# A two-layer decoder trunk on one core: the last layer-norm table loaded earlier, attention masks added on VectorE, state-space tables made dense and spread by ScalarE, and the first weight chunks in pieces

## Chip, cores, metric

One Trainium2 chip, one of its cores. The time is the device time of one execution in microseconds (us); less is better. Before the change it is 2101.03 us, the median of three runs (2099.38, 2101.03, 2104.73).

## What is computed

Two layers over 256 tokens of width 2048, all in float32:

```python
for i in range(DEPTH):                       # DEPTH = 2
    if i % 2 == 0: mix = _even_mixer(x, ...) # u, q, k, v, gate from one projection;
                                             # 8 heads of forgetting attention (causal, with a
                                             # cumulative log gate), a diagonal complex state-space
                                             # layer (S5) with GELU and GLU, one output projection
    else:          mix = _odd_mixer(x, ...)  # 32 query heads, 4 key heads, window 128, sinks, rotary
    x = _layer_norm(ALPHA * x + mix, ...)
    ffn = _conv_ffn(x, ...)                  # 2048 -> 2 x 5504, causal conv of width 3, silu gate, -> 2048
    x = _layer_norm(ALPHA * x + ffn, ...)
```

In the windowed attention the scores outside the band are minus infinity, and the sink of a head is one more logit of its softmax:

```python
s = jnp.where(valid[None, :, None, None], s, -jnp.inf)
p = jax.nn.softmax(jnp.concatenate([s, sink], axis=-1), axis=-1)[..., :-1]
```

## The kernel before

**Weights.** Nearly all time is matmuls with weights that are read once. `Stream` brings them in as chunks, 128 partitions by 1024 columns (512 KB), in the order of the list `items`: SyncE issues the load into a ring of five buffers (`raw`), ScalarE copies the chunk to `hi`, rounded to the matmul's format (L115), VectorE subtracts (`lo = raw - hi`, L120), and TensorE multiplies in three passes: hi with the high half of the activations, hi with the low half, lo with the high half. So 128 rows of a contraction are three matmuls in a row, and one chunk with 512 columns of output is 12. At most `HELD` = 4 chunks are held as hi and lo; chunks whose destination is named ("x", or a place that is free at that time) go there instead. A destination "H" means chunks half as wide (512 columns), cast into a second, narrow set of buffers that `second_buffer` opens.

**Order.** Every engine runs its instructions in the order of the program text as it is executed; there is no scheduler. Work beside the stream comes from generators: after each chunk `done` casts further chunks, as far as there is room, and then `pump` gives each generator a step, which lasts until the costs that the generator yields add up to its budget (`step`, 1.7 for the state-space layer, `S5_BUDGET`), or until it yields 0. So the text's order sets, on each engine, what stands ahead of a cast.

**Stages**, by the timeline: u (16 chunks of wu, to 55 us, tiles of 128 output columns, each from two chunks); the gate (wf, one small chunk) and v (16 chunks of wv) to about 107; q and k with the attention heads, then the output projection's first part, to about 300; GLU and the rest of layer 1's mixer to about 430; its feed-forward net to 1112; layer 2's projections and windowed attention to 1312 and its output projection wo1; the second feed-forward net from 1398; the last down projection's tail and the final layer norm from 2060 on. Between the layers `boundary` runs a layer norm under the matmuls.

**u.** TensorE makes u in two groups of four tiles, for each group first the upper half of the contraction of all four, then the lower. x comes in eight pieces behind the first chunk. A finished tile is copied by ScalarE (L1385) and stored to a scratch tensor (L1386); after each second tile `load_u4` reads the pair back, transposed, with four DMAs that GpSimd issues (L1365).

**State-space layer** (`s5_gen`), one of four groups b after another: `tab` multiplies a phase table with B or C (four products over 128x512 in `z0` to `z3`, then four sums and differences, each over 64 partitions, straight into a sparse, block-diagonal table); `turn` and `kernels` take it through TensorE; GpSimd makes the powers ("phasors", L302 to L304) of which `phase` (six VectorE steps) makes the phases of group b; `toeplitz` fills a table with blocks of a kernel `gs`: four additions with the skip matrix on VectorE and six copies on ScalarE (L1144); `scan` does the recurrence; `emit` the outputs. `weave` places TensorE's parts after a given number of VectorE's steps (`WEAVE`).

**Windowed attention** (`Swa`, `scores` and `soft`), 16 head pairs: six matmuls of q and k into two banks, of 256 and 512 columns, and after each three one matmul of the identity with a mask (`maskr`); two reductions to the negated maximum (L833, L834), a minimum with the sink, and four exponentials on ScalarE from the banks, with their sums (L841). Its output projection wo1 has its chunks of the columns 0 to 1535 from the 17th on as "H".

**The end.** `final` (after the second feed-forward net) opens a buffer, loads scale and bias of the last layer norm, 2 MB, on ScalarE's queue (`load_gb`, L576), and then runs the last eight chunks for each half of the tokens, and the norm.

## Time and profile before

| | us |
|---|---|
| median of three runs | 2101.03 |
| the profiled execution | 2106.23 |
| its span in the profile | 2104.4 |
| TensorE busy | 2071.1 |
| VectorE busy | 1485.5 |
| ScalarE busy | 1144.9 |
| GpSimd busy | 70.7 |

Times of the profile are microseconds from the span's start. PE is TensorE's matmul, PEld its weight load, DVE VectorE, ACT ScalarE, POOL GpSimd, SP SyncE; a trailing q (SPq) is an engine's DMA queue. A row has an engine, a line of the kernel, an operation, and "out<-in" by the names of the tiles without their numbers; a tile without a name is `t`. `bank` is a bank of PSUM. Matmuls overlap, so their durations (0.39 us for 512 columns) add up to more than the time that passes; what one costs is the time from its start to the next one's. In square brackets stands how long the engine sat idle before the row, and what released it.

### The profile page before, as it was taken

How to read it: one execution, taken by the hardware profiler on the slowest of the kernel's cores; microseconds unless marked ns; L12 is line 12 of the kernel's file. 1: busy time of each engine (PE TensorE's matmuls, PEld its weight loads, DVE VectorE, ACT ScalarE, POOL GpSimd, SP SyncE). 2: the span in 40 equal slices, each digit the busy share in tenths (PEclk: the TensorE clock that was granted, in tenths of full speed). 3: DMA queues.
4: the chain of work that ended last, by engine and by line, in shares of the span. 5: the costliest groups of instructions: out<-in, count | busy, mean ns of one | idle time of the engine just before them, and what ended most of it. 6: DMA issues, size and time to landing. Idle time of an engine off the chain costs nothing.

```text
span 2104.4 us, 30826 instructions
## 1 busy us (share of the span) xinstructions
PE 2071.1 (98%) x11228; PEld 1761.9 (84%) x11228; DVE 1485.5 (71%) x2473; ACT 1144.9 (54%) x1920; POOL 70.7 (3%) x140
## 2 busy tenths in 40 slices
PE   8999999999999999999999999999999999999996
PEld 8788878888888888888888877788888888888885
DVE  7898867788777777655557876778777777755555
ACT  5445545665555555544446665475555555544442
POOL 4700000000000000000000000000000000000000
PEclk9999999999999999999999999999999999999998
DMA  8454455576666666466675643657666666646664
GB/s 288 149 166 140 128 194 184 180 220 201 189 189 192 190 189 188 150 188 197 194 240 164 185 127 102 219 182 223 190 189 192 189 190 187 193 148 194 193 193 176
DMA packets 133640, 388.92 MB, mean 185 GB/s; under 512 B 15536, under 2 KB 17584, under 8 KB 133232
## 3 DMA queue, kind: packets, MB, share of 16 engines
q1 hardware_dynamic: 126288, 371.38, 56.7%
q10 hardware_dynamic: 5712, 10.20, 1.9%
q0 software_dynamic: 1488, 5.38, 0.8%
q8 instruction: 88, 1.44, 0.3%
q14 instruction: 64, 0.52, 0.1%
HBM read 383.75 MB, written 3.15 MB: 184 GB/s over the span
## 4 chain that ended last, share of the span: by engine, by line
PE 87%; DVE 5%; DMA 3%; POOL 2%; ACT 2%; issue 1%; SPq 0%; DVEq 0%; ACTq 0%; POOLq 0%
PE bank L242 85%; DVE lo L120 2%; ACT hi L115 1%; DMA raw<-wdn 1%; DVE z L221 1%; DVE t L239 1%; DMA xraw<-xT 1%; POOL t L303 1%; POOL t L304 1%; POOL t L302 1%; DMA t<-ut 1%; DVE t L221 0%; PE bank L521 0%; DMA raw<-wo 0%; DMA raw<-wu 0%
## 5 line engine op out<-in xcount | busy, mean ns | idle before, releaser
L120 DVE TENSOR_TENSOR lo<-raw,hi 128x1024 fp32r<-128x1024 f32 (+1 forms) x828 | 842.7, 1022 | 473.9 <-ACT hi L115 472.8
L242 PE MATMUL bank<-t,hi 128*128 128x512 f32 (+1 forms) x3296 | 1101.1, 385 | 6.9 <-ACT t L115 6.1
L115 ACT CAST hi<-raw 128x1024 fp32r<-128x1024 f32 (+1 forms) x831 | 737.0, 891 | 587.9 <-PE bank L242 323.0
L242 PE MATMUL bank<-t,lo 128*128 128x256 f32 x3152 | 875.9, 278 | 0.9 <-DVE lo L120 0.9
L242 PEld LDWEIGHTS bank<-t,hi 128*128 128x128 f32 x3296 | 610.1, 188 | 138.5 <-ACT t L115 6.1
L242 PE MATMUL bank<-hi,t 128*128 128x512 f32 x2248 | 712.6, 393 | 0.7 <-ACT hi L115 0.7
L242 PEld LDWEIGHTS bank<-t,lo 128*128 128x128 f32 x3152 | 593.2, 188 | 1.8 <-DVE lo L120 1.6
L242 PEld LDWEIGHTS bank<-hi,t 128*128 128x128 f32 x2248 | 422.6, 188 | 94.6 <-issue 3.8
L242 PE MATMUL bank<-lo,t 128*128 128x512 f32 x1124 | 439.7, 391 | 2.0 <-DVE lo L120 2.0
L242 PEld LDWEIGHTS bank<-lo,t 128*128 128x128 f32 x1124 | 211.5, 188 | 47.7 <-DVE lo L120 3.8
L239 DVE SCALAR_TENSOR_TENSOR y<-h,t,y 128x255 f32<-128x255 f32 (+1 forms) x328 | 136.4, 478 | 0.6 <-ACT y L661 0.5
L439 ACT COPY h<-bank 128x256 f32<-128x256 f32 x164 | 60.6, 373 | 88.4 <-PE bank L242 86.0
L661 ACT ACTIVATE y<-h,t 128x256 f32<-128x256 f32 x164 | 90.3, 602 | 13.2 <-DVE h L221 13.0
L242 PE MATMUL bank<-t,t 128*128 128x512 f32 (+3 forms) x422 | 85.6, 349 | 2.1 <-DVE t L239 1.1
L221 DVE TENSOR_TENSOR h<-h,bank 128x256 f32<-128x256 f32 x164 | 67.0, 421 | 21.2 <-ACT h L439 21.2
L242 PEld LDWEIGHTS bank<-t,t 128*128 128x128 f32 (+1 forms) x422 | 61.8, 173 | 14.3 <-DVE t L120 2.2
L841 ACT ACTIVATE p<-bank,sm 128x128 f32<-128x128 f32 (+1 forms) x64 | 26.1, 420 | 45.1 <-DVE sm L221 45.1
L670 ACT ACTIVATE y<-y 128x256 f32<-128x256 f32 x86 | 35.6, 414 | 19.1 <-DVE y L239 19.0
L525 ACT ACTIVATE x<-bank,t 128x128 f32<-128x128 f32 x96 | 36.1, 457 | 10.7 <-PE bank L521 9.3
L245 ACT CAST t<-y 128x256 fp32r<-128x256 f32 x86 | 34.6, 404 | 5.2 <-DVE y L221 5.2
L221 DVE TENSOR_TENSOR t<-y,t 128x256 fp32r<-128x256 f32 x86 | 35.8, 418 | 0.9 <-ACT t L245 0.9
L221 DVE TENSOR_TENSOR y<-y,y 128x256 f32<-128x256 f32 x86 | 35.8, 419 | 0.3 <-ACT y L670 0.3
(172 smaller groups left out, 969.4 us busy)
## 6 DMA issues: line engine op xcount, KB each, us to landing
raw<-wup SPq DMA_DIRECT2D x328, 512.0 KB, 3.7
raw<-wdn SPq DMA_DIRECT2D x292, 256.0 KB, 3.0
raw<-wo SPq DMA_DIRECT2D x56, 512.0 KB, 3.6
raw<-wi SPq DMA_DIRECT2D x40, 512.0 KB, 3.8
raw<-wqk SPq DMA_DIRECT2D x32, 512.0 KB, 3.5
raw<-wdn SPq DMA_DIRECT2D x22, 512.0 KB, 5.1
raw<-wu SPq DMA_DIRECT2D x16, 512.0 KB, 6.4
raw<-wv SPq DMA_DIRECT2D x16, 512.0 KB, 4.1
```

The source lines that it names most:

```text
L115: self.nc.scalar.copy(hi, r)
L120: eng.tensor_tensor(lo, r, hi.bitcast(F32), op=ALU.subtract)
L221: V.tensor_tensor(o, a, b, op=op)
L239: V.scalar_tensor_tensor(o, a, s, b, op0=op0, op1=op1)
L242: PE.matmul(o, lhsT=l, rhs=r, start=start, stop=stop)
L245: S.copy(hi, src)
L302: G.tensor_tensor(t1, a[0], b[i], op=ALU.mult)
L439: S.copy(o, ps[:, T:])
L525: S.activation(x32[:, j], pt[:, j * P:(j + 1) * P], AF.Identity, bias=lnT[:, li, 1, k:k + 1], scale=lnT[:, li, 0, k:k + 1])
L661: S.activation(y[e], ps[e][:, :T], AF.Identity, bias=cw[:, n, 3:4], scale=cw[:, n, 2:3])
L670: S.activation(y[0], y[0], AF.Silu)
L841: S.activation(pp[:, e], vv[:, e], AF.Exp, bias=sm[:, 0, qb, e:e + 1], scale=1.0, accum_out=sm[:, 2, qb, e:e + 1])
```

## The change

It has seven parts.

1. `final` no longer loads the scale and bias. `Ffn.run` does, in the second column block of the last down projection, into the buffer of the transposed activations (`last_gb`).
2. `scores` has no mask matmuls. VectorE adds the mask, which lies in the constants, takes the maximum and writes the sum to SBUF in one `tensor_tensor_reduce` for each head and query block; the sink is its start value. The exponentials work in place.
3. wo1 has only chunks of 1024 columns in the common ring; `second_buffer` isn't opened for it.
4. `tab` makes dense sums and differences over 128 partitions (two instead of four operations), and ScalarE spreads them into the sparse table with four copies. `z0` and `z2` have two buffers. `toeplitz` adds the skip matrix once, in place, and ScalarE copies all ten blocks. The forgetting attention's probabilities are scaled by ScalarE.
5. A generator's rest of budget is carried to its next step (up to twice the budget), for the state-space layer with 1.45 instead of 1.7; `WEAVE` and the first group's places are smaller by what `tab` has lost.
6. The first two chunks of u are loaded and cast in four and two pieces, the first one's between the pieces of x, and four matmuls on zeros go ahead.
7. u's eight tiles are made at once, in eight banks: the upper half of the contraction for all, then the lower half.

```diff
-S5_BUDGET = 1.7
+S5_BUDGET = 1.45
-WEAVE = 2, 3, 5, 7, 8, 11
+WEAVE = 2, 3, 5, 6, 7, 9
...
     def step(self, ent):
         gen, budget = ent
-        spent = 0.0
-        while spent < budget:
+        credit = min(budget + self.credit.get(gen, 0.0), 2 * budget)
+        while credit > 0:
...
+    def piece(i, c, n):
+        m = CH // n
+        items.append((A["wu"][i, 0][:, c * m:(c + 1) * m], m, ("x", ...
+    for h in range(2):
+        for i in range(8):
+            if h == 0 and i < 2:
+                for c in range(4 - 2 * i):
+                    if i == 0:
+                        xchunk(c)
+                    piece(i, c, 4 - 2 * i)
...
-            own = ("H",) if n1 >= 12 + HELD and cc < 3 else None
-            w("wo1", cc, kp, dst=ext("t2", kp, own) if cc == 3 else own)
+            w("wo1", cc, kp, dst=ext("t2", kp) if cc == 3 else None)
...
+    for _ in range(4):
+        PE.matmul(ip[:, :T], lhsT=idle[:, :P], rhs=idle, start=True, stop=True)
...
+                if self.l == 1 and cc == 1:
+                    self.gb = last_gb(3)
...
-            gb = mk(lp, [P, 2, D])
-            load_gb(gb, li, 0, 4)
+        gb, part = ffn.gb, []
...
-                mm(s0, identr, maskr[:, :, 1, :], False, True)
-                mm(s1, identr, maskr.rearrange("p e b k -> p e (b k)"), False, True)
...
+                        V.tensor_tensor_reduce(out=pp[:, e], in0=vv[:, e], in1=cst[:, c:C_CM + P], scale=-1.0,
+                                               scalar=nsk[:, 1, h + e:h + e + 1], op0=ALU.add, op1=ALU.min,
+                                               accum_out=sm[:, 0, qb, e:e + 1])
...
+            for i, f in enumerate((sub, add)):
+                d = x4[2 * i]
+                f(d, d, x4[2 * i + 1])
                 yield 0.6
+                for hf in range(2):
+                    r = slice(64 * hf, 64 * hf + 64)
+                    S.copy(dst[r, i, :, :, 16 * hf:16 * hf + 16], d[r])
...
         def toeplitz(b):
             gs = cell["gs"]
+            add(gs[0:32], gs[0:32], dz[b])
+            yield 0.4
             for q in range(4):
                 for l in range(3 - q, 4):
                     k = l - 3 + q
-                    o = tm[32 * q:32 * q + 32, :, l, :]
-                    if k == 0:
-                        add(o, gs[0:32], dz[b])
-                    else:
-                        S.copy(o, gs[32 * k:32 * k + 32])
-                yield 0.35
+                    S.copy(tm[32 * q:32 * q + 32, :, l, :], gs[32 * k:32 * k + 32])
+                yield 0.1
...
-        ts(pr[:, 0:P], pr[:, 0:P], sm[:, 2, 0:1], ALU.mult)
+        S.mul(pr[:, 0:P], pr[:, 0:P], sm[:, 2, 0:1])
...
-    for i0 in (0, 4):
-        ps = [bank(acc) for _ in range(4)]
-        for c in range(2):
-            for i in range(i0, i0 + 4):
+    ps = [bank(acc if i < 4 else aux) for i in range(8)]
+    for c in range(2):
+        for i in range(8):
```

Three places in the engines' order show what moves. GpSimd, from the loads of the first state-space constants to the first phasors; u_39 and u_42 are the first two pairs of u tiles. Before:

```order
L971 DMA cz_219<-sCz 128x512
L971 DMA dz_220<-sDz 32x256
L1365 DMA u_39_411<-t_164 32x8x64 x4
L1365 DMA u_42_500<-t_164 32x8x64 x4
L302 ISA
L302 TENSOR_TENSOR t_197<-t_197 128x32
```

The change, the same place and, after the line of dots, 24 rows on; the pairs are u_45 and u_48:

```order
L996 DMA dz_247<-sDz 32x256
L1388 DMA u_45_588<-t_187 32x8x64 x4
L309 ISA
L309 TENSOR_TENSOR t_224<-t_224 128x32
...
L310 TENSOR_TENSOR t_224<-t_224 128x32
L311 TENSOR_TENSOR t_224<-t_224 128x32
L1388 DMA u_48_696<-t_187 32x8x64 x4
L309 TENSOR_TENSOR t_231<-t_230,t_224 128x64
```

The second pair's reads have moved from ahead of the phasors to among them.

ScalarE at the end of the v projection, from the cast of chunk 27 (counted from 0) to that of chunk 28. `hi` is a chunk's cast, `gs` the kernel that `toeplitz` copies, the rows of 128x256 and 8x256 the forget gate's tables, and 128x512 the copies of v. Before:

```order
L115 CAST hi_1294<-raw_1080 128x1024
L1301 CAST t_1032<-t_1036 128x256
L1302 CAST t_1033<-t_1036 128x256
L245 CAST t_1034<-bank_1300 128x256
L1305 CAST t_1032<-t_1034 8x256
L1306 ACTIVATE t_1033<-t_1034 8x256
L1305 CAST t_1032<-t_1035 8x256
L1306 ACTIVATE t_1033<-t_1035 8x256
L1144 COPY t_207<-gs_1167 32x8x32 x6
L1410 COPY t_964<-bank_965 128x512
L1410 COPY t_964<-bank_966 128x512
L115 CAST hi_1351<-raw_1140 128x1024
```

The change, from the row behind the cast of chunk 26 to the cast of chunk 28:

```order
L1167 COPY t_234<-gs_1189 32x8x32 x10
L116 CAST hi_1329<-raw_1115 128x1024
L1324 CAST t_1059<-t_1063 128x256
L1325 CAST t_1060<-t_1063 128x256
L252 CAST t_1061<-bank_1335 128x256
L1328 CAST t_1059<-t_1061 8x256
L1329 ACTIVATE t_1060<-t_1061 8x256
L1328 CAST t_1059<-t_1062 8x256
L1329 ACTIVATE t_1060<-t_1062 8x256
L1440 COPY t_984<-bank_985 128x512
L1440 COPY t_984<-bank_986 128x512
L116 CAST hi_1378<-raw_1174 128x1024
```

The Toeplitz copies, ten instead of six, stand ahead of the cast of chunk 27 instead of that of chunk 28.

TensorE at the first head pair's scores; `qT` rows are the products with q, `hi` and `lo` rows those of the weight stream, and t_110 with t_109 the identity with the mask. Before:

```order
L242 MATMUL bank_11440<-hi_11423,t_77 128x512
L242 MATMUL bank_11511<-t_11030,qT_11458 128x256 x3
L242 MATMUL bank_11511<-t_110,t_109 128x256
L242 MATMUL bank_11512<-t_11030,qT_11458 128x512 x3
L242 MATMUL bank_11512<-t_110,t_109 128x512
L242 MATMUL bank_11439<-hi_11453,t_77 128x512
```

The change:

```order
L249 MATMUL bank_11480<-lo_11464,xT_77 128x512
L249 MATMUL bank_11480<-hi_11463,xT_77 128x512
L249 MATMUL bank_11551<-t_11070,qT_11498 128x256 x3
L249 MATMUL bank_11552<-t_11070,qT_11498 128x512 x3
L249 MATMUL bank_11479<-hi_11493,xT_77 128x512
```

The two mask rows are gone, and the stream's next chunk follows the scores at once.

More of the change, by code (lines that the diff above doesn't have):

```diff
@@ L163, in step @@
             if c == 0:
-                return
-            spent += c
+                break
+            credit -= c
+        if gen in self.credit:
+            self.credit[gen] = credit
     def pump(self):
@@ L409, in trunk @@
     identr = mk(const, [P, P], F32R)
-    maskr = mk(const, [P, 2, 2, P], F32R)
+    maskr = mk(const, [P, P], F32R)
     def consts_round():
         S.copy(identr, ident)
-        for e in range(2):
-            S.copy(maskr[:, e, 0, :], cst[:, C_BM:C_BM + P])
-            S.copy(maskr[:, e, 1, :], cst[:, C_CM:C_CM + P])
+        S.copy(maskr, cst[:, C_CM:C_CM + P])
     spare = mk(const, [P, 1])
@@ L423, in warm @@
         S.activation(spare, spare, f)
+    idle = mk(st.xraw, [P, T])
+    V.memset(idle, 0.0)
+    ip = bank(aux)
+    for _ in range(4):
+        PE.matmul(ip[:, :T], lhsT=idle[:, :P], rhs=idle, start=True, stop=True)
     def bmm(ps, hi, lo, k, first, last):
@@ L713, in resid, with last_gb, final, half @@
                 residual(self.ps, 3, (tb,))
[L715 to L744 removed]
+    def last_gb(li):
+        t_ = mk(xtp, [P, KT * 2 * T], tag="xT")[:, :2 * D].rearrange("p (i d) -> p i d", i=2)
+        load_gb(t_, li, 0, 4)
+        return t_
+    def final(ffn):
+        gb, part = ffn.gb, []
+        def half(tb):
+            ffn.resid(tb, 7)
+            steps = ln_stats(tb)
+            next(steps)
+            for c in range(0, D, 256):
+                o = x[:, tb, c:c + 256]
+                stt(o, o, lnw[:, tb, 0:1], gb[:, 0, c:c + 256], ALU.subtract, ALU.mult)
+                next(steps, None)
+            for _ in steps:
+                pass
+            c = 0
+            for n in (512, 512, 512, 256, 256):
+                o = x[:, tb, c:c + n]
+                stt(o, o, lnw[:, tb, 2:3], gb[:, 1, c:c + n], ALU.mult, ALU.add)
+                nc.sync.dma_start(out=out[:, tb, c:c + n], in_=o)
+                c += n
+        for tb in range(2):
+            for c in range(8):
+                if tb == 0:
+                    part.append(st.get())
+                ffn.tail(part[c], tb, c)
+            half(tb)
     rope = mk(const, [P, 2, 2, 8])
@@ L1037, in four @@
         def four(tag="z"):
-            return [mk(wk, [P, 512], tag=f"{tag}{i}") for i in range(4)]
+            return [mk(wk, [P, 512], tag=f"{tag}{i}", bufs=2 - i % 2) for i in range(4)]
         def tab(dst, sc, src, b):
@@ L1226, in s5_gen @@
             if b == 0:
-                yield from weave(tables, (2, turn, 0, 0), (4, turn, 0, 1), (5, kernels, 0, 0), (6, kernels, 0, 1), (8, kernels_turn))
+                yield from weave(tables, (2, turn, 0, 0), (3, turn, 0, 1), (4, kernels, 0, 0), (5, kernels, 0, 1), (6, kernels_turn))
                 while b not in u4:
@@ L1242, in s5_gen @@
             if b < 3:
-                yield from weave((tab(wbs, sb, bt[b + 1], b + 1),), (4, emit, b))
+                yield from weave((tab(wbs, sb, bt[b + 1], b + 1),), (3, emit, b))
             else:
@@ L1528, in trunk @@
     ffn2.hs.close()
-    final(ffn2, 3)
+    final(ffn2)
     ffn2.outer.close()
```

118 lines of the change are left out of this document (48 added, 70 removed).

## The prediction

> **What bounds the kernel now.** I read the page first, then the busy time by stages, then TensorE's timeline at the places where it is not full. The busy totals and the engines of the chain that ended last:
>
> ```profile
> PE 2071.1 (98%) x11228; PEld 1761.9 (84%) x11228; DVE 1485.5 (71%) x2473; ACT 1144.9 (54%) x1920; POOL 70.7 (3%) x140
> PE 87%; DVE 5%; DMA 3%; POOL 2%; ACT 2%; issue 1%; SPq 0%; DVEq 0%; ACTq 0%; POOLq 0%
> ```
>
> TensorE is busy for 98% of the span, so time can go in two ways only: by matmuls that are no longer issued, and by idle stretches of TensorE that close. The stages that the change touches (columns: stretch, length, then busy time and count of PE, PEld, DVE, ACT, POOL, granted clock, DMA share, GB/s):
>
> ```profile
> 58.00:160.00 102.00, 97.68 (x623) 81.86 (x622) 92.68 (x153) 47.58 (x79) 38.07 (x72) 1.00 0.51 158
> 1148.00:1313.00 165.00, 165.00 (x814) 131.09 (x813) 120.02 (x258) 97.96 (x251) 0.00 (x0) 1.00 0.46 137
> 2060.00:2104.00 44.00, 28.40 (x111) 22.00 (x109) 27.18 (x61) 8.07 (x9) 0.00 (x0) 0.83 0.45 170
> ```
>
> In the attention stage (1148 to 1313) TensorE has no gap at all and VectorE 45 us of them. In the state-space stage (58 to 160) TensorE misses 4.3 us and VectorE is the fullest other engine. At the end TensorE stands for a third of the time, at a clock of 0.83.
>
> **The end.** TensorE's timeline there (start, length, last column the idle time and its releaser), then the piece of the chain ahead of it and the two groups of DMA issues:
>
> ```profile
> 2070.01 2.89 PE L242 MATMUL bank<-t 128*128 128x512 f32 x12
> 2076.22 0.79 PE L242 MATMUL bank<-t 128*128 128x512 f32 x1 [3.32 <-ACT t L115]
> 2077.48 3.78 PE L242 MATMUL bank<-t 128*128 128x512 f32 x8 [0.47 <-DVE t L120]
> 2087.25 4.93 PE L242 MATMUL bank<-t 128*128 128x512 f32 x21
> ...
> 2064.46 10.64 DMA raw<-wdn
> ...
> t<-ln ACTq DMA_DIRECT2D x1, 2048.0 KB, 10.7
> ...
> raw<-wdn SPq DMA_DIRECT2D x292, 256.0 KB, 3.0
> ```
>
> `load_gb` in `final` puts 2 MB on ScalarE's queue just when the last weight chunks are asked for. A chunk takes 10.64 us to land, TensorE waits 3.32 and 0.47 us and then goes at half speed: 8 matmuls in 3.78 us, 0.47 each, where later 21 take 4.93, 0.235 each. Without the 2 MB the chunk lands before TensorE has finished its 12 matmuls at 2072.90. From 2076.22 up to 2087.25 it issues 33; at 0.235 they take 7.75 us from 2072.90 and end at 2080.65. **Gain: 2087.25 - 2080.65 = 6.6 us.**
>
> The load goes to the second column block of the last down projection, where chunks of 256 KB stream, six matmuls each. I bound what it does there by two loads of 2 MB: the one above, 6.6 us with its cold clock, and this one in the output projection, with the weight chunks beside it (at other times they take 3.6 us by the page):
>
> ```profile
> raw<-wo SPq DMA_DIRECT2D x4, 512.0 KB, 4.3
> t<-x POOLq DMA_DIRECT2D x1, 2048.0 KB, 10.6
> ```
>
> There no matmul waited. A place with a full ring of chunks ahead is nearer to that one. **Cost: 0 to 6.6, I take 1.4 us.**
>
> **The masks.** 32 matmuls leave the attention scores, half of 512 columns, half of 256:
>
> ```profile
> L242 PE MATMUL bank<-t,t 128*128 128x512 f32 x16 | 6.3, 394 | 0.0
> L242 PE MATMUL bank<-t,t 128*128 128x256 f32 x16 | 4.5, 281 | 0.0
> ...
> L834 DVE TENSOR_REDUCE sm<-bank 128x2 f32<-128x512 f32 x16 | 11.1, 692 | 6.2 <-PE bank L242 6.1
> L841 ACT ACTIVATION_READ_ACCUMULATOR p<-bank,sm 128x1 f32 x64 | 13.0, 203 | 0.0
> ...
> 13.05 0.40 PE L242 MATMUL bank<-t,hi 128*128 128x256 f32 x2
> 13.41 0.40 PE L242 MATMUL bank<-t,hi 128*128 128x256 f32 x2
> ```
>
> Matmuls overlap, so what one is worth is its start-to-start time: 0.235 for 512 columns, and three of 256 every 0.36 us (13.05 to 13.41), 0.12 each. 16 x 0.235 + 16 x 0.12 = 5.7 us, in a stage where TensorE never waits. **Gain 5.5 us**, 4 to 5.7. In their place VectorE does four `tensor_tensor_reduce` per head pair instead of two reductions and a minimum. The trace has no such operation. Two reductions over 512 and 256 columns take 0.69 and some 0.42, so a piece of 128 or 256 columns lies between 0.28 and 0.69, with up to 0.2 to read the accumulator, as ScalarE pays. At the dearest, 4 x 0.9, VectorE gets 2.3 us more for each of 16 pairs, 37 us of its 45 free ones: still hidden. ScalarE's exponentials keep their number and read SBUF instead of PSUM; with 67 of 165 us free they cost nothing.
>
> **The output projection of layer 2** loses its narrow second buffer, whose last chunk came too late:
>
> ```profile
> 1350.61 0.50 PE L242 MATMUL bank<-lo,t 128*128 128x512 f32 x1 [0.88 <-DVE lo L120]
> ```
>
> Twice as wide chunks in the common ring are loaded further ahead. **Gain 1.0 us**, 0 to 1.1.
>
> **The start.** TensorE's first matmuls wait for weights and x:
>
> ```profile
> 6.10 0.58 PE L242 MATMUL bank<-t,hi 128*128 128x256 f32 x1 [6.10 <-ACT t L115]
> 7.44 0.58 PE L242 MATMUL bank<-t,hi 128*128 128x256 f32 x1 [0.76 <-DVE t L120]
> 12.47 0.39 PE L242 MATMUL bank<-t,lo 128*128 128x256 f32 x1 [0.48 <-DVE lo L120]
> ```
>
> Pieces of the first two chunks interleaved with x, and four matmuls on zeros that bring the clock up, are worth 0.76 + 0.48 and part of the slow half up to 10.5 us: 1.9 us, 0.5 to 2.8. But it has to survive the next stage.
>
> **The state-space stage** is where I expect the gain to be lost. GpSimd's timeline, VectorE's, ScalarE's and TensorE's there:
>
> ```profile
> 40.41 2.31 POOL L1365 DMA_DIRECT2D u<-t  x4 [6.42 <-DMA t<-ut]
> 42.81 0.79 POOL L302 TENSOR_TENSOR t<-t 128x32 f32<-128x32 f32 x1
> 89.55 0.46 POOL L304 TENSOR_TENSOR t<-t 128x128 f32<-128x128 f32 x1
> ...
> 90.04 0.71 DVE L221 TENSOR_TENSOR z<-t,t 128x512 f32<-128x512 f32 x1 [1.23 <-POOL t L304]
> 91.39 1.27 DVE L120 TENSOR_TENSOR lo<-raw,hi 128x1024 fp32r<-128x1024 f32 x1
> ...
> 93.31 0.41 ACT L1305 CAST t<-t 8x256 fp32r<-8x256 f32 x1
> 97.06 2.48 ACT L1144 COPY t<-gs 32x256 f32<-32x256 f32 x6
> 99.56 1.07 ACT L1410 COPY t<-bank 128x512 f32<-128x512 f32 x2
> 100.66 3.89 ACT L115 CAST hi<-raw 128x1024 fp32r<-128x1024 f32 x4
> ...
> 97.98 0.61 PE L242 MATMUL bank<-hi,t 128*128 128x512 f32 x2
> 100.70 0.39 PE L242 MATMUL bank<-hi,t 128*128 128x512 f32 x1
> 101.76 0.51 PE L242 MATMUL bank<-hi,t 128*128 128x512 f32 x1 [0.68 <-ACT hi L115]
> ```
>
> I number the weight chunks from 0 (16 of u, one of the gate, 16 of v). TensorE starts chunk 28 at 101.76 after a wait. The two matmuls from 97.98 on are the last of chunk 26 and the first of chunk 27, and its twelfth starts at 100.70: 2.72 / 12 = 0.227 us from start to start. So chunk 27 starts at 98.20 and 26 at 95.48. Already before, this passage is late: VectorE waits 1.23 us for the last phase table, which GpSimd ends at 90.01, and ScalarE casts chunk 28 only after the six Toeplitz copies.
>
> Two things of the change bear on it. First, u tile 1 is complete after the tenth chunk instead of the sixth:
>
> ```profile
> 55.73 0.37 ACT L1385 COPY ut<-bank 128x256 f32<-128x256 f32 x1 [1.00 <-PE bank L242]
> ...
> DMA to landing us min/median/max: 1.9/4.0/6.2
> ```
>
> The last tile is copied at 55.73 and a chunk of 24 matmuls takes 24 x 0.12 = 2.88 us, so the tenth ends at 55.73 - 6 x 2.88 = 38.45, less 1.9 for the start: 36.6. With the copy, 4.0 us for the store and 2.31 for the four reads of `load_u4(0)`, GpSimd begins the phase tables at some 43.8 instead of 42.81; and `load_u4(1)`, 2.31 us, which stood ahead of them, now stands among them. **Tables 3.3 us later: 93.3.** Then VectorE does five 0.7-us steps of the phase, three of them after that moment, and one subtraction: the lower half of chunk 26 is ready at 93.3 + 0.7 + 0.7 + 1.4 + 1.2 = 97.3, where TensorE, 1.9 us ahead, wants it at 94.
>
> Second, ScalarE's order. The sixth phase step (0.7) and one addition over 32x256 (0.4) end at 98.4. The ten Toeplitz copies, 2.48 / 6 = 0.41 each, last until 102.5, and they stand ahead of the cast of chunk 27, which is done at 103.6. TensorE starts chunk 27 at 103.6 instead of 98.20. Behind that cast wait two casts, a copy and four small casts (0.41 each, 2.9 together), two copies of v (1.07) and the cast of chunk 28 (1.05): 108.6, against 101.76. From chunk 29 on the casts follow one another, as before. **Price of the passage: 6 us against before, the start's 1.9 already spent in it**; 3 with tables as early as before (cast of chunk 27 at 100.3), 8 with a store of 6.2 us.
>
> After it VectorE is relieved: per table six operations of 0.7 instead of eight, one addition for four, no scaling of the probabilities; ScalarE takes 32 copies, 16 Toeplitz copies and 16 scalings more, some 32 us of the 54 that it has free in 102. I take **1.5 us gained** of the waits on VectorE up to 430 us, 0 to 3. Slower pacing (1.45 for 1.7, a carried rest) and `WEAVE` only place the same steps; the last one still ends ahead of the GLU weights.
>
> **Sum**, against the profiled execution (span 2104.4, 2106.23 with 1.8 outside it, 5.2 above the median of 2101.03): -6.6 + 1.4 - 5.5 - 1.0 + 6.0 - 1.5 = **-7.2 us**. Taken from the median: **2093.8 us**.
>
> **Rivals.**
> 1. *The passage costs nothing.* GpSimd's steps of one shape differ much:
>
> ```profile
> 74.36 2.32 POOL L304 TENSOR_TENSOR t<-t 128x32 f32<-128x32 f32 x1
> 77.34 0.26 POOL L304 TENSOR_TENSOR t<-t 128x32 f32<-128x32 f32 x1
> ```
>
> If a few of the long ones go as VectorE does less, the tables are not late, and chunks 26 to 28 lose what they lost before. Then the start's 1.9 stays and the 6.0 go: 2093.8 - 7.9 = 2086. For it: the long ones hold over 5 us. Against it: the ten copies ahead of the cast remain, and alone cost 3. In the Trainium skill, GPSIMD Engine Reference, section 1 (Specifications), GpSimd's memory interface is shared with VectorE, with contention when that reads two inputs; the 2.32 beside 0.26 fits, and by that rule fewer two-input operations of VectorE make this rival likelier.
> 2. *The early 2 MB stall TensorE as they did at the end.* Then 6.6 is lost again instead of 1.4: 2099. For it: the same queue and size delayed a chunk by 6 us. Against it: the load beside the output projection. The two rows from 2076.22 on show the price of a pause of 3.8 us: the half clock. The Trainium skill, TensorE: Matmul & The Clock Gate, Part 1, gives an idle window of about 3.4 us that runs freely; the trace agrees, and by it a pause of 1.4 us would mostly keep the clock.
> 3. *VectorE becomes the bound in the attention stage (the slower side).* A pair's part that is replaced takes 1.4 us, 0.36 per new operation, and 45 us are free for 64 of them, 0.7 each: VectorE decides from 1.06 us per operation. At 1.3 it adds 64 x 0.24 = 15 us and TensorE's 5.5 are lost: 2093.8 + 5.5 + 15 = 2114. Against it: no row of that width, with an accumulator, comes near 1.06.
> 4. *The change of the end does nothing,* since the last chunks are late anyway: 2093.8 + 5.2 = 2099. Against it: 3.0 us for a chunk elsewhere.
>
> **Numbers.** This kernel's runs lie within 0.3% (6.3 us) of one another, so that is what counts as no change: from 2094.7 to 2107.3. Forecast 0.50; its sum lies on that bound's faster side by 1 us, so 0.32 of it are faster and 0.18 the same. Rival 1 0.28, faster. Rivals 2 and 4 0.15, the same. Rival 3 0.05, slower. Another stall in the state-space stage 0.02, the same. Faster 0.60, same 0.35, slower 0.05. The range reaches from rival 1 (2086, less 1 for the other bounds) to rivals 2 and 4 (2099, with the 8-us passage 2101): 2085 to 2101.
>
> **What would show it.** Right: TensorE without a gap from 2060 on, and no `bank<-t,t` of 256 or 512 columns in the scores; chunk 27 waited for at about 99 to 104, with the Toeplitz copies ahead of its cast and GpSimd's last 128x128 table at 93; the attention stage shorter by 5 to 6. Wrong: a start of chunk 28 before 103 (rival 1), an idle time of 3 us in the last down projection (rival 2), VectorE at 100% in the attention stage (rival 3).

## The result, and the profile after

The changed kernel takes 2124.95 us, the median of four runs (2123.48 to 2127.25), the one before 2101.62 us beside it (2099.38 to 2104.73): 1.0116 times as long, 95% interval 1.0100 to 1.0132. It is slower by 23 us where 7 us of gain were forecast, outside the range. The profiled execution of the changed kernel took 2127.25 us with a span of 2125.5, 21.1 more than the span of before.

To see where, I compare the start of the same matmul (the n-th that reads a chunk's hi or lo) in the two traces. What each stretch adds to its delay:

| stretch | forecast, us | measured, us | delay at its end |
|---|---|---|---|
| start, u tiles | -1.9 | -1.5 | -1.5 |
| gate, first chunks of v, to 84 us | 0 | -1.5 | -3.0 |
| passage of chunks 26 to 28 and what follows, to 122 us | +7.9 | +5.2 | +2.2 |
| state-space groups 1 to 3 with the attention heads, to 360 us | -1.5 | **+26.8** | +29.0 |
| masks | -5.5 | -5.6 | +23.4 |
| output projection of layer 2 | -1.0 | -0.4 | +23.0 |
| early load of 2 MB | +1.4 | +5.1 | +28.1 |
| end | -6.6 | -7.0 | +21.1 |

One term has the wrong sign and holds all of the loss. The small terms are less sure than they look, since the column compares two single executions and that of before is 5.2 us above its median: in the six kernels below that keep the old end, the last stretch took from 4.5 us less to 0.7 more than in it.

The busy totals, from the page of the changed kernel:

```profile
PE 2083.9 (98%) x11204; PEld 1768.5 (83%) x11204; DVE 1464.5 (69%) x2506; ACT 1176.5 (55%) x1977; POOL 66.7 (3%) x140
```

TensorE is busy for 13 us longer with fewer matmuls, VectorE does less, ScalarE more: as meant, and the time went up. The totals hide why; the stages show it. Busy time by stages, after (columns as in the prediction; the attention stage, 1148 to 1313 before, now lies from 1177 to 1336):

```profile
1177.00:1336.00 159.00, 159.00 (x781) 125.76 (x780) 122.33 (x337) 101.64 (x250) 0.00 (x0) 1.00 0.50 152
104.00:360.00 256.00, 237.34 (x1462) 200.19 (x1461) 169.88 (x245) 140.42 (x259) 4.86 (x9) 0.94 0.44 136
```

The last stretch for the kernel before:

```profile
104.00:360.00 256.00, 250.47 (x1613) 214.73 (x1613) 205.69 (x315) 130.88 (x237) 4.86 (x9) 1.00 0.51 160
```

In 256 us TensorE issues 151 matmuls fewer, is idle for 13 us more, and its granted clock is 0.94 instead of 1.00. By an estimate from these figures the clock costs 0.06 of 256, some 15 us, so the loss of the stage is about half waiting and half lower clock. VectorE is idle for 86 us and ScalarE for 116: neither is full. What TensorE waited for there, after:

```profile
PE bank L249 <- ACT czn L1102: 7.1, 3, 2.9
PE bank L249 <- DVE qk L228: 4.6, 1, 4.6
PE bank L249 <- DVE t L228: 2.1, 1, 2.1
```

and before (us in total, times, longest):

```profile
PE bank L1218 <- ACT u L1205: 2.1, 1, 2.1
PE bank L242 <- DVE t L239: 1.1, 1, 1.1
PE bank L242 <- DVE qk L221: 0.8, 1, 0.8
...
PE bank L242 <- ACT czn L1077: 0.6, 1, 0.6
```

The new waits are on results that pass through ScalarE. `czn` is a negated copy that needs nothing of the tables. The longest wait, 4.57 us, is on a `qk` that VectorE makes from a copy of ScalarE; ScalarE's, VectorE's and TensorE's timelines around it:

```profile
217.48 2.51 ACT L1085 COPY t<-z 64x512 f32<-64x512 f32 x4
220.00 4.12 ACT L1167 COPY t<-gs 32x256 f32<-32x256 f32 x10
224.13 0.37 ACT L460 COPY qk<-bank 128x256 f32<-128x256 f32 x1
```

```profile
216.11 0.40 DVE L228 TENSOR_TENSOR gs<-gs,dz 32x256 f32<-32x256 f32 x1
224.54 0.42 DVE L228 TENSOR_TENSOR qk<-qk,bank 128x256 f32<-128x256 f32 x1 [8.03 <-ACT qk L460]
...
225.10 0.77 PE L249 MATMUL bank<-qk,qk 128*128 128x128 f32 x2 [4.57 <-DVE qk L228]
```

Fourteen copies, 6.6 us, eight more than the kernel before has in these two steps, stand ahead of one copy of 0.37 that two engines wait for. VectorE idles for 8 us in a stage for which I had promised it relief. In that wait and behind it TensorE's clock is halved (the column before the last two):

```profile
223.00:229.60 6.60, 4.33 (x13) 3.62 (x14) 4.41 (x6) 4.13 (x8) 0.00 (x0) 0.50 0.25 74
```

The passage. TensorE's timeline at chunk 27, ScalarE's ahead of it, and GpSimd's first read and last phase table:

```profile
95.75 0.39 PE L249 MATMUL bank<-hi,xT 128*128 128x512 f32 x1
99.62 0.50 PE L249 MATMUL bank<-hi,xT 128*128 128x512 f32 x1 [3.48 <-ACT hi L116]
100.88 0.80 PE L249 MATMUL bank<-lo,xT 128*128 128x512 f32 x1 [0.76 <-DVE lo L121]
...
94.37 4.13 ACT L1167 COPY t<-gs 32x256 f32<-32x256 f32 x10 [9.47 <-DVE gs L228]
98.52 1.04 ACT L116 CAST hi<-raw 128x1024 fp32r<-128x1024 f32 x1
...
41.03 2.34 POOL L1388 DMA_DIRECT2D u<-t  x4 [32.21 <-DMA t<-ut]
88.85 0.46 POOL L311 TENSOR_TENSOR t<-t 128x128 f32<-128x128 f32 x1
```

The ten copies do stand ahead of chunk 27's cast, and TensorE waits for it, as forecast. But GpSimd ends the table at 89.31, earlier than before (90.01), not at 93.3. The 90.01 is itself late for that kernel: in the three kernels below that keep its start and its tables the same table ends at 85.9 to 86.8, since there the second pair's read waits 2.2 to 2.6 us for its store, not the 6.42 of the profile before.

The early load and the end, after: two pieces of the chain, TensorE's timeline where the late chunk is used, and the DMA issue:

```profile
1931.23 9.99 DMA raw<-wdn
...
2069.99 43.45 PE bank L249 x190
```

```profile
1936.22 0.62 PE L249 MATMUL bank<-hi,t 128*128 128x512 f32 x2
...
1936.90 0.62 PE L249 MATMUL bank<-hi,t 128*128 128x512 f32 x2
...
1938.94 0.39 PE L249 MATMUL bank<-hi,t 128*128 128x512 f32 x1
1941.99 0.50 PE L249 MATMUL bank<-hi,t 128*128 128x512 f32 x1 [2.66 <-ACT hi L116]
1942.72 0.50 PE L249 MATMUL bank<-lo,t 128*128 128x512 f32 x1 [0.23 <-DVE lo L121]
1943.06 0.92 PE L249 MATMUL bank<-hi,t 128*128 128x512 f32 x2
...
1944.20 1.05 PE L249 MATMUL bank<-hi,t 128*128 128x512 f32 x2
...
1945.48 1.05 PE L249 MATMUL bank<-hi,t 128*128 128x512 f32 x2
```

```profile
xT<-ln ACTq DMA_DIRECT2D x1, 2048.0 KB, 10.2
```

The stall that was taken from the end, a chunk that needs 10 us, came up at 1931 again, if smaller: 2.89 us of waits, then three matmuls in 1.14 and 1.28 us (1943.06 to 1944.20 to 1945.48) instead of 0.68 (1936.22 to 1936.90). The end itself has no gap: the chain's last 43 us of matmuls are one piece.

### The profile page after: what moved, and what is told of

It is laid out like the page before. It is cut to its first block, busy times and chain, and to the rows that moved or that the text cites. A ratio compares the mean times of both kernels' runs of the same rounds, so it can differ in the third digit from the quotient of the medians.

```text
span 2125.5 us, 30843 instructions
## 1 busy us (share of the span) xinstructions
PE 2083.9 (98%) x11204; PEld 1768.5 (83%) x11204; DVE 1464.5 (69%) x2506; ACT 1176.5 (55%) x1977; POOL 66.7 (3%) x140
## 4 chain that ended last, share of the span: by engine, by line
PE 88%; DVE 4%; ACT 3%; POOL 2%; issue 1%; DMA 1%; SPq 0%; DVEq 0%; ACTq 0%; POOLq 0%
PE bank L249 86%; DVE lo L121 2%; ACT hi L116 1%; DVE t L246 1%; POOL t L309 1%; DMA t<-x 1%; POOL t L310 1%; ACT t L1167 0%; POOL t L311 0%; DMA raw<-wdn 0%; ACT t L1085 0%; POOL u L1388 0%; DVE z L228 0%; PE bank L542 0%; PE bank L883 0%
## 5 line engine op out<-in xcount | busy, mean ns | idle before, releaser
L249 PE MATMUL bank<-xT,hi 128*128 128x512 f32 (+1 forms) x3264 | 1100.9, 388 | 0.0
L249 PE MATMUL bank<-xT,lo 128*128 128x256 f32 x3136 | 874.2, 279 | 0.2 <-DVE lo L121 0.2
L249 PEld LDWEIGHTS bank<-xT,hi 128*128 128x128 f32 x3264 | 607.8, 189 | 133.0 <-issue 1.7
L249 PEld LDWEIGHTS bank<-xT,lo 128*128 128x128 f32 x3136 | 593.4, 189 | 1.0 <-DVE lo L121 0.8
L249 PE MATMUL bank<-hi,t 128*128 128x512 f32 x1672 | 526.5, 394 | 4.8 <-ACT hi L116 2.7
L249 PEld LDWEIGHTS bank<-hi,t 128*128 128x128 f32 x1672 | 315.6, 189 | 75.6 <-ACT hi L116 3.1
L249 PE MATMUL bank<-lo,t 128*128 128x512 f32 x836 | 328.2, 393 | 0.2 <-DVE lo L121 0.2
L249 PE MATMUL bank<-hi,xT 128*128 128x512 f32 x576 | 191.2, 400 | 3.5 <-ACT hi L116 3.5
L249 PEld LDWEIGHTS bank<-hi,xT 128*128 128x128 f32 x576 | 109.5, 190 | 28.8 <-ACT hi L116 3.9
L249 PE MATMUL bank<-lo,xT 128*128 128x512 f32 x288 | 113.9, 396 | 1.2 <-DVE lo L121 1.2
L249 PEld LDWEIGHTS bank<-t,xT 128*128 128x128 f32 x192 | 35.5, 188 | 10.2 <-DVE t L121 2.2
```

The lines of the kernel that those rows point to most:

```text
L249: PE.matmul(o, lhsT=l, rhs=r, start=start, stop=stop)
```

## The experiments

The theory was that the loss sits in the state-space and attention parts (dense tables with spreading copies, new Toeplitz, scaling on ScalarE, places and pace), because ScalarE, in order, now stands between VectorE and TensorE (a hop, in what follows). Rivals were the start with its order of u, and the early load.

### All of the state-space and attention parts undone

```diff
-S5_BUDGET = 1.45
+S5_BUDGET = 1.7
-WEAVE = 2, 3, 5, 6, 7, 9
+WEAVE = 2, 3, 5, 7, 8, 11
...
-                    S.copy(dst[r, i, :, :, 16 * hf:16 * hf + 16], d[r])
+                sub(dst[r, 0, :, :, o], x4[0][r], x4[1][r])
...
-        S.mul(pr[:, 0:P], pr[:, 0:P], sm[:, 2, 0:1])
+        ts(pr[:, 0:P], pr[:, 0:P], sm[:, 2, 0:1], ALU.mult)
```

> The change with its state-space and forget-attention parts as before (sums of the tables into the sparse form on VectorE, four Toeplitz additions, scaling on VectorE, budget 1.7 without a carried rest, the old WEAVE); masks, start, u by halves, wo1 and the early 2 MB stay changed. Theory (the loss of 29 us up to 430 us sits in these parts): 2125 less 27 to 30 us, so 2094 to 2098, with TensorE's shift against the kernel before at 430 us back at -3 to +1. Rival 1 (the loss comes from u by halves and the late pairs of u tiles): no faster than 2115. Rival 2 (the double z buffers or the memory layout): the same, above 2115.

Measured: 2096.9 us, 0.9982 of before (0.9972 to 0.9991), 28 less than the changed kernel. The loss is in these parts, and not in the doubled buffers of `z0` and `z2`, which this kernel keeps. The passage shows something more; GpSimd's read and last table, and TensorE, in this kernel:

```profile
41.49 2.34 POOL L1388 DMA_DIRECT2D u<-t  x4 [32.68 <-DMA t<-ut]
90.89 0.45 POOL L309 TENSOR_TENSOR t<-t 128x128 f32<-128x128 f32 x1
...
103.08 0.51 PE L247 MATMUL bank<-hi,xT 128*128 128x512 f32 x1 [3.00 <-ACT hi L116]
```

With the tables of before the last phase table ends at 91.34, 1.3 later than before, and the start's gain is lost in the passage (the delay goes from -1.5 to +1.7). With the dense tables it ended 2.0 us earlier, although the read that opens it moved by 0.5 only. That fits the first rival's reason. So do the kernels with the old order of u: from its first table step to this table's end GpSimd takes 44.3 to 46.2 us in the four with dense tables, 47.1 to 47.6 in the five with the tables of before, the kernel before among them. The Trainium skill, GPSIMD Engine Reference, section 1 (Specifications), has GpSimd contend with VectorE's two-input operations; the trace agrees in direction.

### One part undone at a time

The tables with their places (same lines as above, without the rest); the scaling:

> The change with only the tables as before (four half-partition sums and differences on VectorE, no spreading copies on ScalarE, old WEAVE). Theory A (the spreading copies stand on ScalarE ahead of what TensorE waits for: 7 us of waits for czn in the trace, plus the half clock after them): 2125 less 12 to 20, so 2105 to 2113, no wait for czn over 1 us. Theory B (the scaling of the probabilities on ScalarE): less than 4 us faster. Theory C (the pacing): less than 4 us faster.

> The change with only the scaling of the forget attention's probabilities back on VectorE. Theory B (ScalarE's scaling, behind casts, delays the transposes of the probabilities, 1.8 us at 158.8 and the q, k wait of 4.6 us at 220): 2125 less 8 to 15. Theory A (the tables): less than 4 us faster. Theory C (the pacing): less than 4 us faster.

The pace, `S5_BUDGET = 1.7` and no carried rest:

> The change with only the pacing back (budget 1.7, no carried rest), WEAVE as changed. Theory C (the carried rest lets steps pile up, up to twice the budget, ahead of casts): 2125 less 10 or more. Theory A or B: within 5 us of 2125, on either side.

The tables and the pace together:

> The change with the tables and the pacing as before, Toeplitz copies and scaling on ScalarE as changed. Theory A (the tables' way through ScalarE is the cause; undoing it alone left the state-space layer late, at the slower pace, and TensorE waited for its GELU): 2097 to 2103, the shift against the kernel before under 6 us at 430 us. Rival (Toeplitz copies and scaling carry a good part): above 2108.

The Toeplitz step:

```diff
-            add(gs[0:32], gs[0:32], dz[b])
-            yield 0.4
...
-                    S.copy(tm[32 * q:32 * q + 32, :, l, :], gs[32 * k:32 * k + 32])
-                yield 0.1
+                    if k == 0:
+                        add(o, gs[0:32], dz[b])
+                    else:
+                        S.copy(o, gs[32 * k:32 * k + 32])
+                yield 0.35
```

> The change with only the Toeplitz table as before (four additions on VectorE, six copies on ScalarE). The prediction's term (ten copies ahead of the cast of chunk 27): the wait at about 96 us 1.6 us shorter, 2125 less 1 to 4. Rival (the Toeplitz copies carry the loss of groups 1 to 3 too): less 10 or more.

Measured, all from the changed kernel (2124.95):

| undone | us | ratio to before (95%) |
|---|---|---|
| tables and places | 2118.44 | 1.0086 (1.0071 to 1.0101) |
| scaling | 2123.38 | 1.0104 (1.0087 to 1.0121) |
| pace | 2130.94 | 1.0148 (1.0131 to 1.0164) |
| tables, places and pace | 2102.55 | 1.0012 (1.0000 to 1.0024) |
| Toeplitz | 2105.92 | 1.0022 (1.0012 to 1.0031) |

The parts don't add up. The tables gave back less than I had expected (2105 to 2113), the Toeplitz step far more (1 to 4 us less). The scaling is next to nothing. The pace fits the new tables (without it 6 us more are lost) and hurts the old ones (2118.44 against 2102.55): with the tables of before the slower pace brings the state-space layer late to the GLU, where TensorE then waits 6.0 us for `u`. The Toeplitz step takes 19 us with it, among them the whole passage: with it undone the delay is -3.1 at 84 us and -3.0 at 122. So in the changed kernel the ten copies are the passage's price, as the prediction had them.

### Places, engine and price inside the changed kernel

The step that reads the new table moved three steps back; the spreading copies on GpSimd; a Toeplitz row that costs its generator what it cost before:

```diff
-WEAVE = 2, 3, 5, 6, 7, 9
+WEAVE = 5, 6, 7, 8, 9, 11
```

> The change with one line different: WEAVE = 5, 6, 7, 8, 9, 11 instead of 2, 3, 5, 6, 7, 9, so that TensorE's kernels of groups 1 to 3 stand three VectorE steps, some 1.5 chunks, behind the spreading copies. Theory A (TensorE reaches the kernels while the copies still wait in ScalarE's order; the hop has no slack): waits for czn below 1 us in all, 2125 less 6 to 14. Rival (ScalarE has too much to do in this stage, wherever TensorE's parts stand): within 4 us of 2125, or slower.

```diff
-                    S.copy(dst[r, i, :, :, 16 * hf:16 * hf + 16], d[r])
+                    G.tensor_copy(dst[r, i, :, :, 16 * hf:16 * hf + 16], d[r])
```

> The change with the 32 spreading copies on GpSimd instead of ScalarE. Theory A, if it is ScalarE's queue of casts ahead of the copies that delays them: waits for czn gone, 2125 less 6 to 14. If it is the hop itself, whichever engine makes it: GpSimd is slower and shares its port with VectorE, so 2125 less 3 to plus 8.

```diff
-                yield 0.1
+                yield 0.35
```

> The change with one number different: toeplitz yields 0.35 after each of its four rows of blocks instead of 0.1, so that the pacer no longer lets all ten copies (4.1 us of ScalarE) out in one step; the ten copies and the one addition stay. Theory D (it is the burst, issued in one step ahead of casts, of the q copy and of the scaling): most of what the old Toeplitz table gave back, so 2104 to 2112. Rival (it is ScalarE's amount of work, 4 copies more per group): within 4 us of 2125.

Measured: 2114.11 (1.0061, 1.0039 to 1.0084), 2124.91 (1.0119, 1.0090 to 1.0148), 2114.81 (1.0053, 1.0038 to 1.0068). Later places give 11 us back: TensorE's waits for `czn` fall from 7.1 to 0.8. The price of before for a row gives 10: fewer copies are let out in one step, and the longest wait for a `qk` falls from 4.6 to 1.6. GpSimd in ScalarE's place seems to give nothing, but the trace shows two effects that cancel. Groups 1 to 3, 122 to 360 us, cost 12.3 us instead of 26.8, and the passage 0.5 instead of 5.2. A new loss stands ahead of them: the four copies of the first group's table stand in GpSimd's order behind its phase tables, and TensorE waits for them from 65 to 79 us:

```profile
PE bank L1094 <- POOL t L1085: 13.2, 1, 13.2
```

So taking the copies off ScalarE helps where they held up its casts, and another engine in between is a hop as well, with an order of its own.

### One part alone in the kernel before

The new Toeplitz step alone, then the dense tables with their copies, buffers and places alone:

> The kernel before with the new Toeplitz table alone (one addition, ten copies on ScalarE, yields 0.4 and 0.1). Theory D with the interplay (the burst costs a stall only where the tables' copies and the scaling stand on ScalarE beside it): 2101 plus 1 to 5, nearly all of it at 96 to 104 us. If the burst alone carries the loss: 2101 plus 12 or more.

> This is the kernel before with the dense tables alone: two wide operations of VectorE per table, four spreading copies on ScalarE, the doubled buffers and the table list's places 2, 3, 5, 6, 7, 9; the Toeplitz copies, the scaling of the probabilities, the pacing, the start and the end are those of before. Kernel before: 2101 to 2102 us. Theory A (the parts lose together: each adds a little to the same queue of ScalarE, and only the sum outruns the casts): tables alone cost little, as the new Toeplitz alone did (+1 to +3), 2102 to 2108 us, and TensorE's waits for czn between 104 and 360 us add up to less than 4 us. Rival B (the tables' hop through ScalarE loses by itself): at least 15 us of the 26 are there without any other part, 2116 us or more, with waits for czn of 2 to 3 us in each of the groups 1 to 3.

Measured: Toeplitz 2105.44 us (1.0015, 1.0006 to 1.0024), tables 2122.84 us (1.0113, 1.0098 to 1.0128). The ten copies alone cost little in the passage, where I had expected their price: the delay goes from -0.3 at 84 us to -1.3 at 122, and from -0.7 to -2.8 in the last kernel below, which has the same start and six copies. In both the phase table ends early, at 86.8 and 86.6. My theory that only all of them together lose fell here: the tables alone lose 22 us, as much as the whole change. TensorE's waits from 104 to 345 us with the tables alone:

```profile
PE bank L242 <- ACT czn L1077: 5.7, 3, 2.2
PE bank L242 <- DVE t L239: 5.5, 2, 2.8
PE bank L242 <- DVE qk L221: 3.7, 5, 1.1
```

Four kernels take this apart. The new places without the tables (`WEAVE` and the other places of the change):

> The kernel before with nothing but the new places (the list 2, 3, 5, 6, 7, 9, the first group's 2, 3, 4, 5, 6 and 3 for the last step of a group); tables, copies and buffers as before. The kernel before: 2100 to 2102 us. Theory A (the tables lose because TensorE's steps that read them wait for ScalarE's spreading copies, which stand in order with casts and negations): without the copies the earlier places cost little, 2098 to 2106 us, and waits for czn between 104 and 360 us stay under 2 us. Rival B (the places themselves are too early for the chain of table, kernel and turn): 2110 us or more with the old tables too.

The tables alone with their reader three steps later (`WEAVE = 5, 6, 7, 8, 9, 11`):

> The kernel before with the dense tables alone, as in the run of the tables by themselves (2122.8 us), but with the list at 5, 6, 7, 8, 9, 11: the step that reads the new table stands three phase steps of VectorE further behind the copies. Theory A (the distance between the copies and their reader is what is short): most of the 22 us goes, 2102 to 2110 us, and TensorE waits for czn less than 2 us. Rival C (the copies lose wherever their reader stands, by holding up the casts behind them on ScalarE): 2117 us or more, with TensorE's waits moved to hi and lo of the chunks.

The tables alone, with the copies on VectorE:

```diff
-                    S.copy(dst[r, i, :, :, 16 * hf:16 * hf + 16], d[r])
+                    V.tensor_copy(dst[r, i, :, :, 16 * hf:16 * hf + 16], d[r])
```

> The kernel before with the dense tables and new places as in the run of the tables by themselves (2122.8 us), but the spreading copies done by VectorE, which so computes a table alone, without a hop to ScalarE. VectorE then has more work than before: 24 copies of about 0.6 us between 104 and 345 us for 12 half additions of 0.68 fewer, some 7 us more of the 50 it has free there. The kernel before: 2100 to 2102 us. Theory A (the hop to ScalarE and back is what loses, not the amount of work): 2102 to 2110 us, the places' own 4 us among them, and VectorE's idle time for ScalarE's casts between 104 and 345 us near the 30 of before instead of 55.7. Rival (the dense form loses by itself, by its buffers or its longer steps): 2115 us or more.

The tables with ScalarE's copies, but eight yields per table and all places as before, so that every matmul stands in TensorE's order where it stood:

```diff
             for i, f in enumerate((sub, add)):
                 d = x4[2 * i]
                 f(d, d, x4[2 * i + 1])
                 yield 0.6
                 for hf in range(2):
                     r = slice(64 * hf, 64 * hf + 64)
                     S.copy(dst[r, i, :, :, 16 * hf:16 * hf + 16], d[r])
+                yield 0.6
```

> The kernel before with the dense tables and ScalarE's spreading copies, but with the steps of before: a table yields eight times as it did (after each wide operation, and again after its two copies), and the list and the other places are those of before, so that TensorE's steps stand where they stood. The kernel before: 2099 to 2102 us. Theory A (the table loses because its steps no longer stand for its work: six yields for ten operations put more of them between two casts, and the places moved with them): 2101 to 2108 us. Rival B (the hop through ScalarE loses wherever it stands): 2115 us or more, with VectorE's idle time for ScalarE's casts between 104 and 345 us near 50 instead of 30.

Measured:

| kernel before with | us | ratio to before (95%) |
|---|---|---|
| places alone | 2105.45 | 1.0021 (1.0009 to 1.0033) |
| tables, reader later | 2123.52 | 1.0103 (1.0079 to 1.0128) |
| tables, copies on VectorE | 2115.53 | 1.0073 (1.0056 to 1.0090) |
| tables, eight yields, old places | 2114.50 | 1.0054 (1.0035 to 1.0074) |

The reader's distance is not it: with it later the waits for `czn` go (0.5 us left) and as many come elsewhere. TensorE's waits there, same stretch:

```profile
PE bank L242 <- DVE t L239: 6.0, 2, 3.2
PE bank L242 <- DVE qk L221: 5.5, 5, 1.9
```

The last kernel is the cleanest, since TensorE's order is that of before, and still 12 us are lost. Its waits for `czn` were 0.6 us before:

```profile
PE bank L242 <- ACT czn L1078: 6.8, 3, 2.7
```

The first of them, with ScalarE ahead of it:

```profile
123.75 1.25 ACT L1060 COPY t<-z 64x512 f32<-64x512 f32 x2 [2.22 <-DVE z L221]
125.02 1.05 ACT L115 CAST hi<-raw 128x1024 fp32r<-128x1024 f32 x1
125.97 1.24 ACT L1060 COPY t<-z 64x512 f32<-64x512 f32 x2
127.24 1.07 ACT L1411 COPY t<-bank 128x512 f32<-128x512 f32 x2
128.34 1.04 ACT L115 CAST hi<-raw 128x1024 fp32r<-128x1024 f32 x1
129.29 0.41 ACT L1078 ACTIVATE czn<-cz 128x256 f32<-128x256 f32 x1
...
129.75 0.66 PE L242 MATMUL bank<-t,czn 128*32 128x128 f32 x8 [2.75 <-ACT czn L1078]
```

The same place in the kernel before:

```profile
122.64 1.05 ACT L115 CAST hi<-raw 128x1024 fp32r<-128x1024 f32 x1
123.59 0.42 ACT L1077 ACTIVATE czn<-cz 128x256 f32<-128x256 f32 x1
```

ScalarE waits 2.22 us for VectorE's wide operation and copies for 2.49; two casts and `czn`, which need nothing of it, stand behind. Shown so far: of the 22 us of the tables some 12 come with TensorE's order unchanged. Most of that can be put down to the hop: 6.2 us more of waits for `czn`, and two stretches of 3.4 us at half clock, in or behind two of these waits. The doubled buffers are in this kernel too, but cost nothing in the kernel with all these parts undone. Some 8 to 10 more come with fewer yields and earlier places: the tables alone lose 8 us less with the old yields and places (2122.84 to 2114.50), and 4 are lost by the places alone. Copies on VectorE save 7 of the 22; that is less than I had expected of the hop (2102 to 2110) and within the rival's range. VectorE's idle time for ScalarE's casts, 30.1 us before and 55.7 with the tables alone, is 38.6 with eight yields and 35.8 with the copies on VectorE. The other 15 us of that last kernel are only in part explained. A wait of 2.73 us for VectorE, at 116.37, stands in all four kernels with the new places (at 113.28 in the one with the places alone) and is 1.1 in the kernel before; the delay grows by 5.7 us there. The rest may be its two more operations per table, which no yield counts; that stays open.

### The early load and better versions

From the kernel with the state-space parts undone, the early load in four pieces of 512 KB, one every seven chunks (the expectation says eight; the edit and the trace have seven); then also u in two groups of four tiles as before; then, from the kernel before, masks, common buffers, the doubled `z0` and `z2` and eight loads of 256 KB, one every five chunks:

```diff
+        def pieces():
+            for q in range(4):
+                load_gb(t_[:, :, 512 * q:512 * q + 512], li, q)
+                for _ in range(7):
+                    yield 0
+        st.add(pieces())
```

> The change with its state-space and forget-attention parts as before (2096.9 so far) and the early 2 MB in four loads of 512 KB, one every eight weight chunks of the second column block. Theory (the one load of 2 MB holds up the chunk asked for beside it by 7 us, as it did at the end): no wait for a chunk between 1880 and 1950, 1 to 4 us faster than with one load: 2093 to 2096. Rival (any early load takes the same bandwidth from the chunks): no difference.

> As gb_pieces, and u in two groups of four tiles as before (the first pairs of u tiles after the sixth and the eighth chunk), with the first chunks still in pieces. Theory E (with u by halves GpSimd's tables come later against TensorE, and the start's gain is lost in waiting for chunk 28): the start's 1.5 us stays, 2 to 3 us faster than gb_pieces: 2089 to 2093. Rival (the tables stay where they are and the passage takes back what the start gives in any case): within 1 us of gb_pieces.

> The kernel before with the masks on VectorE, the common buffers in layer 2's output projection, and scale and bias of the last layer norm in eight loads of 256 KB, one after every fifth chunk of the last down projection; start and state-space layer as before. Kernel before: 2101 to 2102 us. Theory A (a load no larger than a chunk, at a fifth of the chunks' rate, fits between them): the gains are 7 at the end, 5.6 in the attention and 0.4 in the output projection, with 0 to 1 lost to the loads: 2088 to 2090 us. Rival B (every such load delays the chunk beside it whatever its size, as four of 512 KB did): 3 to 5 us are lost there, 2092 to 2095 us, and TensorE's waits of 0.3 to 2 us stand in the last down projection.

Measured: 2097.81 (0.9972, 0.9961 to 0.9983), 2094.70 (0.9958, 0.9942 to 0.9975), 2092.49 (0.9962, 0.9947 to 0.9978). All three beat both kernels, and all three stayed above what my theories had (2093 to 2096, 2089 to 2093, 2088 to 2090; the last lies within its rival's 2092 to 2095); the first is no faster than the kernel with one load (2096.9). The load cost 3.65, 2.2 and 1.6 us there; in one piece it cost 1.3 with the state-space parts undone and up to 5.1 in the other kernels that have it. The DMA issues of the four-piece and of the eight-piece load:

```profile
xT<-ln ACTq DMA_DIRECT2D x4, 512.0 KB, 7.1
```

```profile
xT<-ln ACTq DMA_DIRECT2D x8, 256.0 KB, 4.5
```

A quarter of the bytes takes 0.7 of the time. Pieces of 512 KB don't help; that 256 KB do is likely, not shown, since one piece has cost as little once. With u in two groups the passage no longer loses (delay +0.7 at 84 us, 0.0 at 122; with u by halves +0.1 and +2.1), and the phase table ends at 90.02 instead of 91.74, so the order of u makes the phase tables later. But the start's gain, which was to stay, isn't there: the delay is +0.7 at 55 us.

## Why the prediction was wrong, step by step

- **The failed step:** "After it VectorE is relieved ... ScalarE takes 32 copies, 16 Toeplitz copies and 16 scalings more, some 32 us of the 54 that it has free in 102. I take 1.5 us gained." It was +26.8 us. Free time was taken as cover. The amount was about right (ScalarE is busy for 31.6 us more) and ScalarE has that time, but its order has no slack: copies that wait for VectorE, or that come ten at a time, hold up casts, `czn` and `qk` that have nothing to do with them, and around TensorE's waits for those its clock is halved. The two together are about 13 us more of idling and 15 of lower clock between 104 and 360 us. Rows that were at hand spoke against it: TensorE's few waits of before already were on results that came by ScalarE or VectorE. The step's sentence on pacing and `WEAVE`, that they "only place the same steps", fell with it: places and price are worth 4 to 11 us in the runs. No rival had this mechanism either; the slower side's rival was in another stage, and "another stall in the state-space stage" had a chance of 0.02, as no change of time.
- **The passage** was right in its mechanism (ten copies ahead of chunk 27's cast, a wait at 99.62) and 2.7 us too dear in size: 5.2 instead of 7.9. The step "tables 3.3 us later: 93.3" came out at 89.31 in the changed kernel and at 91.34 without the dense tables. Its base, 90.01, was one late execution; against the 85.9 to 86.8 of the three kernels with the same start and tables, 91.34 is some 5 us later. (Its "43.8" is a slip too: its own terms give 43.3, and GpSimd began at 43.47.) The first rival's reason held, its result did not, because the ten copies remained ahead of the cast, as it said: its price of 3 us is 4.9 with the start's 1.9, against 5.2 measured.
- **The start:** -1.5 for -1.9, where seven kernels with the old start differ from before by -0.7 to +0.4. Further 1.5 us came before the passage, which no term had.
- **The masks:** -5.6 for -5.5, with VectorE at 122.33 of 159 us. What a new operation costs, after:

```profile
L861 DVE CUSTOM_DVE_ANT_0 p<-bank,t,t 128x256 f32<-128x256 f32 x32 | 14.2, 480 | 0.6
L861 DVE CUSTOM_DVE_ANT_0 p<-bank,t,t 128x128 f32<-128x128 f32 x32 | 9.9, 347 | 10.5 <-PE bank L249 10.4
L861 DVE DVE_READ_ACCUMULATOR2_ANT sm<- 128x1 f32 x64 | 5.2, 82 | 0.0
```

  0.43 and 0.56 us with the accumulator's read, within the bounds and far from the third rival's 1.06.
- **The early load:** 5.1 for 1.4, inside its bounds of 0 to 6.6. The nearer row was the wrong one to lean on; over the kernels that have it in one piece it costs 1.3 to 5.1, the more the later the chunk beside it lands (after 7.8 us for the 1.3, after 10.0 for the 5.1) and by whether the clock falls. The second rival happened, in size and form, and was masked by the loss elsewhere. By the idle window of about 3.4 us that the Trainium skill, TensorE: Matmul & The Clock Gate, Part 1, gives, a pause shorter than that keeps the clock. The trace differs: a wait of 2.66 us was followed by the half clock. Length alone doesn't decide it: at the same place a wait of 2.96 us with the tables undone kept the full clock, and one of 2.08 with the Toeplitz price of before did not.
- **The end:** -7.0 for -6.6, and the fourth rival is out. That the two sizes are so near is in part luck: both use the one profiled execution of before, and against the six other kernels with the old end the gain is 2.4 to 7.5 us. **The output projection:** -0.4 for -1.0, within its bounds of 0 to 1.1.

## What to carry to other kernels

Before moving work to an engine that is "free for 54 us", look at what stands behind the new instruction in its order and who waits for that: an operation that depends on another engine's fresh result blocks everything behind it, however short it is. Where generators place work by declared costs, a move between engines changes what a step stands for; price it anew, or the steps bunch up. And test each part of a bundle alone, and undone: here three parts that gain 13 us were hidden by a group that loses 27. In that group the tables alone lose 22 and the Toeplitz step alone 3, yet undoing the Toeplitz step gave back 19.

## What the runs showed that I had not expected

- Giving a chain of copies to a third engine (GpSimd for ScalarE) left the time as it was, 2124.91 for 2124.95 us, though the trace is another: one wait of 13.2 us came, and the stage that had lost 26.8 us lost 12.3.
- A broadcast load of 512 KB beside the stream of chunks takes 7.1 us, one of 2048 KB 10.2.
- A wait of TensorE of 2.66 us was followed by matmuls at half speed (1.28 us for three instead of 0.68); in another kernel one of 2.96 was not.
- GpSimd's phase tables ended 2 us earlier (89.31 for 91.34) when VectorE did fewer two-input operations beside them; 0.5 of it is an earlier start.
